# The bonus term of a time-mix layer: scale and offset applied where each direction's gate is taken up

## Chip, cores and metric

One core of one Trainium2 chip runs the whole program. The metric is device microseconds (us) of one launch: the median of three runs. The engines are called as the profile calls them: PE (TensorE matmul), PEld (its weight loads), DVE (VectorE), ACT (ScalarE), POOL (GpSimd), SP (SyncE, which here issues the DMAs).

## The reference, cut to what matters

The model is a trunk of two layers (a Mamba-2 mixer, then an RWKV-7 time mix), applied to 512 and 256 tokens of 1024 channels. Only the time mix is touched. For each of two directions z it computes a gate `a`, a key `k_dir` that depends on the gate, and, beside the recurrent scan, a bonus term, which sums over both directions:

```
a     = sigmoid(a0 + la @ a_up)                       # one gate for each direction z
k_dir = k * (1 + (a - 1) * k_a)
bonus = sum_over_z( sum_over_channels_of_a_head( r * k_dir * r_k ) ) * v
out   = ((y + bonus) * g) @ w_out
```

Both directions have the same r, k and r_k, so the sum over z needs the sum of the two gates only. With a = (1 + t) / 2, t being a tanh, the factor on r * k is rkk0 * (t_forward + t_backward) + rkk1, where rkk0 = k_a * r_k / 2 and rkk1 = (2 - k_a) * r_k are columns with one value for each channel.

## The kernel before

The 1024 channels of the time mix are eight blocks b of 128 channels (two heads of 64), with channels on the partitions and the 768 tokens along the free axis. For each block the program has five parts:

- `rwkv_in(b)`: the dense projections of k, r, v and g (fp32 as three fp32r products, lines 140 to 142 in `mm3`), shifted by a token (L737, L739) and stored to DRAM; q, k and r come back from there as `Wr`.
- `p1(b)`: six windows of 256 tokens, three for each direction. `p1_front` makes the decay (`ld`, `EP`) and the gate's tanh `ta` (L876); `p1_back` makes the matrices that the scan needs: `G` (POOL, L901 and L903), `KB` (ACT L897, DVE L898 and L904), `TD` and the rest of `G` from the product `ptd` (PE L912, DVE L914 and L917), `BK` (L922, L923). At its end stands the bonus term (L925 to L939).
- `rwkv_inverse(b)`: inverts the 24 triangular matrices of a block, mostly by a long row of small DVE operations (L963, L964), between DVE transposes (L956, L966, L967) and PE products (L977, L986).
- `chain_step(b, 0..7)`: the scan itself, a chain PE `pr` -> ACT `R` -> PE `pS` -> DVE and ACT `SV` -> PE `pz` -> DVE (L1017, L1031, L1056, L1057, L1065), with outputs `py` (L1039) copied to `Y` (L1076).
- `rwkv_final(b)`: the statistics of a block's output, `Y` added, centred, squared and scaled (POOL L1090, L1094, L1095, L1100; DVE L1093, L1097, L1098 and the reciprocal root `ng` in L103 to L108), then transposed by PE as `pf` (L1104), the bonus added (L1113), the gate g multiplied in (L1114).

The bonus in detail. The tile `ts` holds 768 tokens. Of the six windows three are the first to touch their 256 tokens (`first`), three the second. The first copies its `ta` to `ts` (ACT L927). The second adds its own `ta` (POOL L929), applies scale and offset rkk0 and rkk1 (DVE L930), multiplies by r and k (POOL L931, then L933 twice on 64 partitions), sums over each head with a product by `bones` (PE L935), multiplies by v (DVE L938) and stores to DRAM (L939). With eight blocks each of these lines runs 24 times, L933 and (as two passes) L935 48 times. The result is read back only in `rwkv_final(b)`, after the block's eight chain steps.

The order of the instructions on each engine isn't that of the code. After the program is written, a planner (`arrange`, `Program.schedule`) gives every instruction a cost by engine, operation and size, follows the dependencies, and lists the instructions of each engine by priority, in several passes with several settings; the best list by its own costs is fixed. Its lists are the order of issue on every engine, SP's DMAs included, so a changed cost or a vanished instruction at one place can move instructions anywhere in the program, the Mamba layer too. Dense products (the projections of later blocks, the output product) fill PE between the chain's small products.

Of the kernel before, what the change touches and what calls it, by code (L numbers as in the profile page):

```python
# [18 lines left out]
AF = mybir.ActivationFunctionType  # L19
ALU = mybir.AluOpType  # L20
# [28 lines left out]
def bc(ap, axis, n):  # L49
    a = ap.unsqueeze(axis)  # L50
    s = list(a.shape)
    s[axis] = n
    return a.to_broadcast(s)
# [6 lines left out]
class Trunk:  # L60
# [824 lines left out]
    def p1_back(self, b, w, z, o, a, ps4, first, W, En, ta, EP):  # L885
        nc = self.nc
        col = lambda t, i: t[:, i, b : b + 1]
        G, TD, PC = self.G, self.TD, self.PC[b]
        w4 = lambda ap: ap.rearrange("p (c t) -> p c t", t=C)
        m4 = bc(self.maskc[:, z].rearrange("p a t -> p (a t)"), 1, 4)  # L890
        flat = lambda ap: ap.rearrange("p c a t -> p c (a t)")
        tok = lambda ap: ap[..., ::-1] if z else ap
        pc = PC[:, 4 * w : 4 * w + 4]
        KB = self.wt([P, 4, 2, C], "KB")
        kv = KB.rearrange("p c j t -> p j c t")
        for j in range(2):
            nc.scalar.activation(kv[:, j], w4(ta), AF.Identity, scale=col(self.sx, 2 * j), bias=col(self.sx, 2 * j + 1))  # L897
        nc.vector.tensor_mul(kv, kv, tok(W[:, 0:2]).rearrange("p j (c t) -> p j c t", t=C))  # L898
        for h in range(2):
            hr = HR[h]  # L900
            nc.gpsimd.tensor_tensor(G[hr, ps4, h, 0, :], EP[hr, :, 0:C], w4(tok(W[hr, h])), op=ALU.mult)  # L901
            rho = G[hr, ps4, h, 1, :]
            nc.gpsimd.tensor_tensor(rho[..., ::-1] if z else rho, EP[hr, :, 1:], w4(tok(W[hr, 2])), op=ALU.mult)  # L903
        nc.vector.tensor_mul(kv, kv, bc(w4(En), 1, 2))  # L904
        nc.gpsimd.tensor_copy(pc, EP[:, :, C])


        ps = self.pt("s", [P, 2, 4, 2 * C], "ptd")
        for c in range(4):
            g = G[:, ps4.start + c * ps4.step]  # L910
            for h, j in ((0, 0), (1, 0), (0, 1), (1, 1)):
                nc.tensor.matmul(ps[HR[j], h ^ j, c], KB[HR[h], c, j], g[HR[h], h].rearrange("p a t -> p (a t)"),  # L912
                                 start=True, stop=True)
        nc.vector.tensor_tensor(flat(TD[:, ps4]), ps[:, 0], m4, op=ALU.mult)  # L914
        for h in range(2):
            hp = HR[1 - h]
            nc.vector.tensor_tensor(flat(G[hp, ps4, h]), ps[hp, 1], m4[hp], op=ALU.mult)  # L917
        for c in range(4):
            nc.scalar.activation(KB[:, c], KB[:, c], AF.Copy, scale=pc[:, c : c + 1])  # L919
        ps = self.pt("mi", [P, 4, 2 * C], "pbk")  # L920
        for c in range(4):
            nc.tensor.transpose(ps[:, c, :], KB[:, c].rearrange("p j t -> p (j t)"), self.ident)  # L922
        nc.scalar.copy(flat(self.BK[:, ps4]), ps)  # L923

        ts = self.ts[:, a : a + 256]  # L925
        if first:
            nc.scalar.copy(ts, tok(ta))  # L927
        else:
            nc.gpsimd.tensor_add(ts, ts, tok(ta))  # L929
            nc.vector.tensor_scalar(ts, ts, col(self.rkk, 0), col(self.rkk, 1), op0=ALU.mult, op1=ALU.add)  # L930
            nc.gpsimd.tensor_mul(ts, ts, W[:, 2])  # L931
            for h in range(2):
                nc.gpsimd.tensor_mul(ts[HR[h]], ts[HR[h]], W[HR[h], 1 - h])  # L933
            ps = self.pt("mi", [P, 256], "pbo")
            nc.tensor.matmul(ps, self.bones, ts, start=True, stop=True)  # L935
            v = self.rw.tile([P, 256], F32, tag="bo", bufs=1, name="v")
            nc.sync.dma_start(v, self.vin[b][:, a : a + 256])
            nc.vector.tensor_mul(ts, v, ps)  # L938
            nc.sync.dma_start(self.bod[b][:, a : a + 256], ts)  # L939
# [990 lines left out]
```

## Time and profile before

| what | value |
|---|---|
| median of three runs | 1632.25 us (1629.48 to 1632.38) |
| profiled execution, its own time | 1634.65 us |
| its span, first to last instruction | 1632.9 us |
| mean granted PE clock in it | 0.961 of full speed |
| PEld busy | 1293.0 us (79%) |
| DMA | 161.41 MB, mean 99 GB/s |
| time-mix layer | from about 785 us to the end |

An engine's busy time counts its instructions, not its waits, and a mean busy share mixes stages. A row of a group gives line, engine, operation, tiles out<-in, shapes and count, then its total us and the mean ns of one, then the idle time just before it with what ended that. In a timeline row stand the start, the duration, the engine and line, and in brackets the idle time before it and who ended that.

### The profile page before, as it was taken

The page shows a single profiled execution, that of the slowest core. Times are in us where ns is not written, and L with a number is a line of the kernel's source. Part 1 is how long each engine was busy: PE and PEld are TensorE (multiplying, and loading weights), DVE is VectorE, ACT ScalarE, POOL GpSimd, SP SyncE. Part 2 cuts the span into 40 slices and gives each one's busy share as a digit, 9 for nine tenths or more (in the row PEclk, how much of TensorE's full clock was granted, in tenths as well). Part 3 has the DMA queues.
Part 4 walks back from the last instruction along what each step waited for, and adds up shares of the span by engine and source line. Part 5 has one row for each costly group of instructions (what it writes and reads, how often), then busy time and mean ns, then how long its engine had stood idle before and what let it go on. Part 6 is the DMA issues. An engine that isn't in the chain of part 4 may idle for free. (4 is left out here: it accounts for less than half of the span.)

```text
span 1632.9 us, 39446 instructions
## 1 busy us (share of the span) xinstructions
PE 1526.4 (93%) x15210; PEld 1293.0 (79%) x15210; DVE 1361.9 (83%) x3031; ACT 850.8 (52%) x1980; POOL 723.5 (44%) x1007
## 2 busy tenths in 40 slices
PE   7999999999999899999979989999898999988996
PEld 6888888888988689998758767777777777776885
DVE  6779988888888885668688898989989898989768
ACT  4345444544545352424464757657574757656332
POOL 1168465574574661000070836446372836547210
PEclk9999999999999899999988898999899999979998
DMA  5110211212112044513334343443434344354332
GB/s 175 54 47 26 78 40 59 72 65 72 56 36 85 13 143 143 182 53 110 120 109 132 94 122 107 116 140 101 139 88 126 113 121 126 102 159 137 97 111 85
DMA packets 150316, 161.41 MB, mean 99 GB/s; under 512 B 39632, under 2 KB 106928, under 8 KB 150128
## 3 DMA queue, kind: packets, MB, share of 16 engines
q1 hardware_dynamic: 150128, 158.89, 32.5%
q8 instruction: 120, 1.97, 0.5%
q14 instruction: 68, 0.56, 0.1%
HBM read 121.43 MB, written 40.55 MB: 99 GB/s over the span
## 5 line engine op out<-in xcount | busy, mean ns | idle before, releaser
L140 PE MATMUL pj<-xh,whi 128*128 128x256 f32 (+1 forms) x1056 | 384.7, 365 | 18.9 <-ACT whi L122 10.2
L142 PE MATMUL pj<-xh,wlo 128*128 128x256 f32 (+1 forms) x1056 | 381.1, 361 | 4.3 <-DVE wlo L123 4.3
L141 PE MATMUL pj<-xl,whi 128*128 128x256 f32 (+1 forms) x1056 | 378.3, 358 | 1.4 <-DVE xl L136 1.4
L140 PEld LDWEIGHTS pj<-xh,whi 128*128 128x128 f32 x1056 | 207.0, 196 | 50.6 <-ACT whi L122 10.3
L142 PEld LDWEIGHTS pj<-xh,wlo 128*128 128x128 f32 x1056 | 207.3, 196 | 30.6 <-DVE wlo L123 6.2
L141 PEld LDWEIGHTS pj<-xl,whi 128*128 128x128 f32 x1056 | 207.7, 197 | 27.0 <-DVE xl L136 2.0
L122 ACT CAST whi<-wraw 128x512 fp32r<-128x512 f32 x213 | 131.4, 620 | 125.2 <-PE pj L141 61.7
L123 DVE TENSOR_TENSOR wlo<-wraw,whi 128x512 fp32r<-128x512 f32 x213 | 159.9, 755 | 33.3 <-ACT whi L122 31.1
L414 POOL TENSOR_SCALAR G<-past,ddt,dt 128x128 f32<-128x128 f32 x192 | 136.2, 720 | 84.6 <-DVE ddt L320 57.8
L140 PE MATMUL po<-whi,xh 128*128 128x256 f32 x528 | 151.8, 288 | 1.5 <-DVE acc L501 1.5
L142 PE MATMUL po<-whi,xl 128*128 128x256 f32 x528 | 152.0, 288 | 0.0
L141 PE MATMUL po<-wlo,xh 128*128 128x256 f32 x528 | 151.5, 287 | 0.0
L234 DVE SCALAR_TENSOR_TENSOR conv<-conv,convw 128x770 f32<-128x770 f32 x128 | 140.7, 1099 | 1.3
L140 PE MATMUL pz<-whi,xh 128*128 128x256 f32 x384 | 113.9, 297 | 1.1 <-DVE sz L258 1.1
L378 POOL TENSOR_TENSOR xw<-xB,dtws 128x256 f32<-128x256 f32 x64 | 53.5, 845 | 135.8 <-ACT xB L366 126.3
L901 POOL TENSOR_TENSOR G<-EP,Wr 64x256 f32<-64x256 f32 x96 | 88.5, 922 | 56.7 <-DMA Wr<-ind 36.3
L142 PE MATMUL pz<-whi,xl 128*128 128x256 f32 x384 | 111.5, 290 | 0.0
L141 PE MATMUL pz<-wlo,xh 128*128 128x256 f32 x384 | 111.1, 290 | 0.0
L140 PEld LDWEIGHTS po<-whi,xh 128*128 128x128 f32 x528 | 100.8, 191 | 2.9 <-DVE acc L501 1.9
L141 PEld LDWEIGHTS po<-wlo,xh 128*128 128x128 f32 x528 | 100.9, 191 | 1.5 <-issue 0.3
L142 PEld LDWEIGHTS po<-whi,xl 128*128 128x128 f32 x528 | 100.6, 191 | 1.5 <-DVE xl L136 0.2
L903 POOL TENSOR_TENSOR G<-EP,Wr 64x256 f32<-64x256 f32 x96 | 89.4, 931 | 1.7 <-ACT KB L919 0.8
(274 smaller groups left out, 3837.9 us busy)
## 6 DMA issues: line engine op xcount, KB each, us to landing
wraw<-in_r_w_in SPq DMA_DIRECT2D x72, 256.0 KB
Wr<-ind SPq DMA_DIRECT2D x48, 384.0 KB
wraw<-in_m_w_xbc SPq DMA_DIRECT2D x64, 256.0 KB
wraw<-in_m_w_z SPq DMA_DIRECT2D x32, 256.0 KB
wraw<-in_m_w_out SPq DMA_DIRECT2D x32, 256.0 KB
ydram<-yst SPq DMA_DIRECT2D x16, 384.0 KB
yraw<-ydram SPq DMA_DIRECT2D x24, 256.0 KB
ind<-k SPq DMA_DIRECT2D x32, 192.0 KB
```

The costliest lines, as they stand in the source:

```text
L122: nc.scalar.copy(hi, raw)
L123: nc.vector.tensor_sub(lo, raw, hi.bitcast(F32))
L140: mm(ps, ah, bh, start=first, stop=False)
L141: mm(ps, ah, bl, start=False, stop=False)
L142: mm(ps, al, bh, start=False, stop=last)
L234: nc.vector.scalar_tensor_tensor(acc, u[:, t : t + n], w[:, b, t : t + 1], acc, op0=ALU.mult, op1=ALU.add)
L378: nc.gpsimd.tensor_tensor(hv(xw), hv(xB[c][:, 0:256]), bc(self.dtws[:, c, z, hs], 2, 64), op=ALU.mult)
L414: nc.gpsimd.tensor_scalar(G[:, h, :], self.past, self.ddt[:, c, i : i + 1], self.dt[:, c, 0, i : i + 1], op0=ALU.mult, op1=ALU.add)
L901: nc.gpsimd.tensor_tensor(G[hr, ps4, h, 0, :], EP[hr, :, 0:C], w4(tok(W[hr, h])), op=ALU.mult)
L903: nc.gpsimd.tensor_tensor(rho[..., ::-1] if z else rho, EP[hr, :, 1:], w4(tok(W[hr, 2])), op=ALU.mult)
```

## The change

Scale and offset are applied where a gate is taken up. The first window's copy becomes an ACT activation with a scale and a bias for each partition (rkk0 and rkk1). The second window's two instructions become one DVE instruction, which multiplies `ta` by rkk0 and adds `ts`. POOL's addition is gone. All later lines stand one line higher (L931 becomes L930, L1104 becomes L1103).

```diff
         ts = self.ts[:, a : a + 256]
         if first:
-            nc.scalar.copy(ts, tok(ta))
+            nc.scalar.activation(ts, tok(ta), AF.Identity, scale=col(self.rkk, 0), bias=col(self.rkk, 1))
         else:
-            nc.gpsimd.tensor_add(ts, ts, tok(ta))
-            nc.vector.tensor_scalar(ts, ts, col(self.rkk, 0), col(self.rkk, 1), op0=ALU.mult, op1=ALU.add)
+            nc.vector.scalar_tensor_tensor(ts, tok(ta), col(self.rkk, 0), ts, op0=ALU.mult, op1=ALU.add)
             nc.gpsimd.tensor_mul(ts, ts, W[:, 2])
             for h in range(2):
                 nc.gpsimd.tensor_mul(ts[HR[h]], ts[HR[h]], W[HR[h], 1 - h])
```

`tok` reverses the tokens for the backward direction; `col(t, i)` is one column of 128 values.

The planner's lists change on all five engines. On POOL in block 0, where `p1(0)` makes its `G` with nothing else to run, there stood in the middle of the windows (rows in order of issue, tiles out<-in, then partitions by elements):

```order
L901 TENSOR_TENSOR G<-EP,Wr 64x4x64
L903 TENSOR_TENSOR G<-EP,Wr 64x4x64
L929 TENSOR_TENSOR ts<-ts,ta 128x256
L901 TENSOR_TENSOR G<-EP,Wr 64x4x64
L903 TENSOR_TENSOR G<-EP,Wr 64x4x64
L901 TENSOR_TENSOR G<-EP,Wr 64x4x64
L931 TENSOR_TENSOR ts<-ts,Wr 128x256
L903 TENSOR_TENSOR G<-EP,Wr 64x4x64
L933 TENSOR_TENSOR ts<-ts,Wr 64x256 x2
```

At the same place of POOL's list there now stands:

```order
L903 TENSOR_TENSOR G<-EP,Wr 64x4x64
L930 TENSOR_TENSOR ts<-ts,Wr 128x256
L905 COPY PC<-EP 128x4
L932 TENSOR_TENSOR ts<-ts,Wr 64x256
L901 TENSOR_TENSOR G<-EP,Wr 64x4x64
L903 TENSOR_TENSOR G<-EP,Wr 64x4x64
L901 TENSOR_TENSOR G<-EP,Wr 64x4x64
L903 TENSOR_TENSOR G<-EP,Wr 64x4x64
L932 TENSOR_TENSOR ts<-ts,Wr 64x256
```

The addition is gone from the run of `G`. The three products of the bonus (L930 and L932, before L931 and L933) are still in it; two of them now stand ahead of the four `G` of a window which they stood among or behind before.

The second place is DVE in the statistics of block 1, between the first and the second step of the reciprocal root (L108 writes `ngy` at the end of each step), while L963 and L964 invert the matrices of block 2, L123 splits weights and L739 shifts projections. The list before, up to the second L108:

```order
L123 TENSOR_TENSOR wlo<-wraw,whi 128x512
L963 TENSOR_TENSOR XN<-TL,tl 128x220
L106 TENSOR_TENSOR ngh<-ngy 128x12
L964 TENSOR_TENSOR tl<-tl,XN 128x11x20
L107 SCALAR_TENSOR_TENSOR ngh<-ngh,gv 128x12
L123 TENSOR_TENSOR wlo<-wraw,whi 128x512
L963 TENSOR_TENSOR XN<-TL,tl 128x210
L739 SCALAR_TENSOR_TENSOR rv<-pj_12315,hmu,rv 128x255
L964 TENSOR_TENSOR tl<-tl,XN 128x10x21
L739 SCALAR_TENSOR_TENSOR rv<-pj_12315,hmu,rv 128x255
L963 TENSOR_TENSOR XN<-TL,tl 128x198
L108 SCALAR_TENSOR_TENSOR ngy<-ngh,ngy 128x12
```

Between the same two steps the changed list has:

```order
L108 SCALAR_TENSOR_TENSOR ngy<-ngh,ngy 128x12
L962 TENSOR_TENSOR XN<-TL,tl 128x210
L106 TENSOR_TENSOR ngh<-ngy 128x12
L963 TENSOR_TENSOR tl<-tl,XN 128x10x21
L107 SCALAR_TENSOR_TENSOR ngh<-ngh,gv 128x12
L962 TENSOR_TENSOR XN<-TL,tl 128x198
L108 SCALAR_TENSOR_TENSOR ngy<-ngh,ngy 128x12
```

(L962 and L963 are now what L963 and L964 were.) Eleven rows stood between the two steps, now five: the two weight splits and the two shifts stand ahead of the first step, two rows of the inverse behind the second. None of these rows belongs to the bonus.

## The prediction

> **What bounds the kernel now.** I read the page's busy times first, then the stretches of the time-mix layer one by one, then who waits for whom, then single rows.
>
> ```profile
> PE 1526.4 (93%) x15210; PEld 1293.0 (79%) x15210; DVE 1361.9 (83%) x3031; ACT 850.8 (52%) x1980; POOL 723.5 (44%) x1007
> ```
>
> PE comes first over the whole span, POOL last. But the change lies after 785 us, so the stretches matter (columns: length, then busy us of each engine with its instructions, granted PE clock, DMA share, GB/s):
>
> ```profile
> core 0: us, PE busy (x) PEld busy (x) DVE busy (x) ACT busy (x) POOL busy (x), PEclk, DMA share, GB/s
> 814.00:850.00 36.00, 25.69 (x284) 19.81 (x283) 31.86 (x45) 24.32 (x64) 31.01 (x45) 0.81 0.35 103
> 1000.00:1500.00 500.00, 464.46 (x6252) 369.34 (x6252) 449.48 (x1009) 326.85 (x817) 274.45 (x405) 0.94 0.41 119
> 1155.00:1170.00 15.00, 10.89 (x44) 8.37 (x43) 14.56 (x48) 2.64 (x6) 2.20 (x2) 0.77 0.46 141
> 785.00:1633.00 848.00, 767.26 (x9638) 623.35 (x9636) 729.77 (x1752) 498.69 (x1240) 386.04 (x573) 0.93 0.40 117
> ```
>
> Three regimes. From 814 to 850 us, the first block's windows, POOL and DVE are nearly full and PE waits. In the blocks that follow PE and DVE share the bound (93% and 90% of 1000 to 1500 us) and POOL has 45% to spare. In the last 15 us of a block's statistics (1155 to 1170) DVE is full, PE has 4 us of holes and its clock is at 0.77. The waits say which hole is largest (who waited for whom, us, times, longest):
>
> ```profile
> PE pf L1104 <- POOL Y L1100: 18.1, 7, 4.3
> PE tl L977 <- DVE TC L967: 4.2, 3, 2.5
> PE ptd L912 <- POOL G L903: 1.1, 3, 0.4
> POOL Y L1100 <- DVE ngy L108: 43.1, 4, 12.5
> POOL ts L931 <- DVE ts L930: 13.3, 9, 3.6
> ```
>
> PE's largest wait in this layer is for the normalised output before its transposition, 18.1 us in seven blocks, and that waits for the reciprocal root on DVE. The bonus appears only as a wait of POOL, which isn't the bound. For the matrices `G` PE waits 1.1 us in all. So the bonus itself is off the path nearly everywhere; what it does is take time on engines, and occupy a place in lists.
>
> **POOL: 24 additions go.** The groups of the old and the neighbouring lines:
>
> ```profile
> L929 POOL TENSOR_TENSOR ts<-ts,ta 128x256 f32<-128x256 f32 x24 | 20.1, 837 | 3.1 <-ACT ta L876 2.0
> L930 DVE TENSOR_SCALAR ts<-ts,rkk 128x256 f32<-128x256 f32 x24 | 12.1, 503 | 0.6 <-POOL ts L929 0.5
> L927 ACT COPY ts<-ta 128x256 f32<-128x256 f32 x24 | 9.6, 403 | 1.6 <-DMA bod<-ts 1.5
> L897 ACT ACTIVATE KB<-ta,sx 128x256 f32<-128x256 f32 x96 | 53.6, 597 | 7.0 <-PE pbk L922 6.7
> L938 DVE TENSOR_TENSOR ts<-v,pbo 128x256 f32<-128x256 f32 x24 | 9.9, 412 | 2.0 <-PE pbo L935 1.3 <-PE pS L1017 0.3
> L739 DVE SCALAR_TENSOR_TENSOR rv<-pj,hmu,rv 128x255 f32<-128x255 f32 x32 | 15.2, 475 | 0.1
> ```
>
> POOL loses 24 x 0.837 = 20.1 us. Where POOL is 55% busy that is free; in the first block it isn't. There POOL runs back to back:
>
> ```profile
> 824.82 0.69 POOL L903 TENSOR_TENSOR G<-EP,Wr 64x256 f32<-64x256 f32 x1
> 825.58 0.72 POOL L929 TENSOR_TENSOR ts<-ts,ta 128x256 f32<-128x256 f32 x1
> 826.27 1.12 POOL L901 TENSOR_TENSOR G<-EP,Wr 64x256 f32<-64x256 f32 x1
> ```
>
> ```profile
> L929 POOL TENSOR_TENSOR ts<-ts,ta x24: 722/732/1892, 825.6 to 1492.0; 128x256 f32<-128x256 f32 x24
> ```
>
> One addition of 0.72 us stands among the `G`; the other two of the block follow the last `G`. PE, TD, the inverse and the first chain step wait for these `G`. The new list moves two of the bonus's products ahead of one window's `G`, but the last `G` of the block has the same products ahead of it as before, less the addition. Term one: **-0.7 us**. A loss is excluded, since nothing was put into this run; at most it is the longest addition's 1.9 us (least, median, largest ns stand in the last row), if DVE, the other full engine, gives way too.
>
> **DVE: one row for one row.** The old instruction costs 24 x 0.503. The trace has no such operation on two SBUF tiles; the nearest are L938 at 0.412 (two inputs, no pointer) and L739 at 0.475 (a pointer, one input from PSUM). I take L739, being the same operation, and the spread that the old one had above its own median:
>
> ```profile
> L930 DVE TENSOR_SCALAR ts<-ts,rkk x24: 364/406/867, 827.5 to 1501.3; 128x256 f32<-128x256 f32 x24
> L904 DVE TENSOR_TENSOR KB<-KB,ld x48: 654/1052/1254, 814.8 to 1489.5; 128x512 f32<-128x512 f32 x48
> L901 POOL TENSOR_TENSOR G<-EP,Wr x96: 671/946/2503, 814.2 to 1490.2; 64x256 f32<-64x256 f32 x96
> ```
>
> 0.475 + (0.503 - 0.406) = 0.57, so 24 x 0.07 = +1.7 us. Against it stands what the vanished additions took from others: L904 takes between 0.65 and 1.25 us, and POOL's L901 between 0.67 and 2.5, because the two engines hinder each other on SBUF. L904 (mean 0.941, below) loses 48 x (0.941 - 0.654) = 13.8 us over 386 us of POOL; with the two rows
>
> ```profile
> L904 DVE TENSOR_TENSOR KB<-KB,ld 128x512 f32<-128x512 f32 x48 | 45.2, 941 | 0.7
> L898 DVE TENSOR_TENSOR KB<-KB,Wr 128x512 f32<-128x512 f32 x48 | 42.9, 894 | 10.0 <-DMA Wr<-ind 7.7 <-ACT KB L897 1.7
> ```
>
> and the same least time, L898 adds 48 x 0.24 = 11.5 us: 25.3 / 386 = 0.066 us for each us of POOL, 1.3 us for 20.1. Term two: 1.7 - 1.3, of which only a part is on the path: **0**, ends -3.5 (the 0.412 row and the whole relief) and +1.7. The new row waits for ACT's `ta` and for the first window's `ts`, both older than POOL's sum, for which DVE waited 0.5 us in all; so nothing behind it on DVE (most often `TD` or a scan of the next window) gets a wait. No DMA is added or taken away.
>
> The Trainium skill, "SBUF — State Buffer", section "SBUF: two separate sides", says that a VectorE instruction with two SBUF inputs and a GpSimd instruction that reads SBUF exclude each other for a whole instruction. By this rule the new row, with `ta` and `ts` from SBUF, is such a holder 24 times; the trace shows the hindrance, though L930 at up to 0.87 us was hindered with one input already. Its result is a rival below.
>
> **ACT.** The copy becomes an activation with two pointers, as L897 is: 24 x (0.597 - 0.403) = +4.7 us on an engine that is 65% busy from 1000 to 1500 us. Its cover is that slack. In the new list six of the 24 have one of the chain's or the output's copies within the next two rows, so the loss is at most 6 x 0.19 = 1.2 us. Term three: **0**, end +1.2; a gain is excluded, the row only grows.
>
> **What the planner moved.** The lists differ on every engine; three differences can be priced. First, PE turns between the tiled products (L912, L1017, L1039) and full ones 522 times in the old list, 508 times in the new. The price is in four rows:
>
> ```profile
> 1580.41 0.28 PE L142 MATMUL po<-whi,xl 128*128 128x256 f32 x1
> 1580.53 0.28 PE L140 MATMUL po<-whi,xh 128*128 128x256 f32 x1
> 1580.74 0.33 PE L1039 MATMUL py<-SV,TD 64*64 64x64 f32 x4
> 1581.00 0.39 PE L141 MATMUL po<-wlo,xh 128*128 128x256 f32 x1
> 1581.22 0.28 PE L142 MATMUL po<-whi,xl 128*128 128x256 f32 x1
> ```
>
> Dense rows start every 0.12 us; into the tiled row it takes 0.21, out of it the next 0.22: about 0.1 for a turn. Term four: 14 x 0.1 = **-1.4 us**, ends 0 (they fall into holes) and -2.8.
>
> Second, the statistics. From the sums (L1093) to the root's last row the old DVE list has 41 rows in block 0 and 295 in seven blocks, the new one 259.
>
> ```profile
> 963.81 0.95 DVE L1093 TENSOR_REDUCE gm<-Y 128x12 f32<-128x768 f32 x1 [0.39 <-POOL Y L1090]
> 977.35 0.16 DVE L108 SCALAR_TENSOR_TENSOR ngy<-ngh,ngy 128x12 f32<-128x12 f32 x1
> ```
>
> 13.5 us for 41 rows, 0.33 each: 36 rows fewer bring the output 11.9 us earlier in all, against 18.1 us of waiting, less what covers it: the dense rows between the last `py` and the first `pf` come to 79.7 us before and 78.8 now, by the spacings 0.12 above and 0.23 for 512 columns:
>
> ```profile
> 1058.05 0.39 PE L140 MATMUL pj<-xh,whi 128*128 128x512 f32 x1
> 1058.27 0.39 PE L141 MATMUL pj<-xl,whi 128*128 128x512 f32 x1
> ```
>
> That would be -11.0. But DVE is full there, and the rows taken out stand behind the root, where PE waits for the inverse next (L977, 4.2 us already). So most of the wait should move from `pf` to the inverse and not vanish: I take some eighth part, **-1.5 us**, with the ends -11 and +4.3 (the slower rival).
>
> Third, the end. Behind the last chain step the new lists have 28 PE rows and, on DVE, three weight splits (0.75 by the row below) and two accumulations (0.42) less; they now run before it.
>
> ```profile
> L123 DVE TENSOR_TENSOR wlo<-wraw,whi 128x512 fp32r<-128x512 f32 x213 | 159.9, 755 | 33.3 <-ACT whi L122 31.1
> L501 DVE SCALAR_TENSOR_TENSOR acc<-acc,po 128x256 f32<-128x256 f32 x72 | 30.0, 417 | 28.4 <-PE po L142 26.8 <-DMA acc<-x2d 1.3
> ```
>
> The full DVE of the last 30 us saves 3.1, the chain before it meets 28 x 0.12 = 3.4 of dense work: **0**, ends -3.1 and +3.4.
>
> **Sum**: -0.7 - 1.4 - 1.5 = -3.6 us. The profiled execution took 1634.65 us, span 1632.9, so the same execution would take 1631.05; it lies 2.4 above the median 1632.25, which becomes 1628.65, **1628.7 us**. A measurement of this kernel tells about 0.2%, 3.3 us, from no change.
>
> **Rivals.**
>
> *The moved waits come back, no change.* For it: DVE is 97% busy in the statistics, and the turns may fall into the holes of PE. Against: POOL's place in block 0 is real. Only term one is left: 1631.6.
>
> *Faster by far: POOL and DVE exclude each other, and the hole at `pf` closes.* By the lock of whole instructions, each of the 24 additions that meets a holder costs DVE up to 0.73, half on average: 24 x 0.37 = 8.8 us of DVE, of which the 10% of the layer's time that PE idles says little is on the path. With a third of the 11 us of statistics it would be 1628.7 - 0.9 - 2.2 = 1625.6; with all 11 and no return, 1618. For it: L904's median of 1.05 against a least of 0.65. The rule named above would make it so, if the new rows weren't holders too.
>
> *Slower: the statistics are no earlier, and blocks 1 and 3 have less to cover them.* Dense rows ahead of `pf` come to 10.9, 11.7, 11.4, 12.3, 11.2, 10.9, 11.3 us by block before, and 10.7, 10.2, 13.2, 10.2, 10.7, 12.1, 11.6 now. If POOL's and ACT's steps, and not DVE's rows, set when the output is ready, the four blocks that lose cover pay 4.3 us, and those that gain get nothing where the inverse is next to be late: 1632.25 + 4.3 = 1636.6. It decides once the statistics gain less than some 0.6 us a block. A hole also costs clock:
>
> ```profile
> 1066.25 0.27 PE L801 MATMUL prs<-ident,nky 128*12 128x128 f32 x1 [1.77 <-DVE rv L739]
> 1067.90 0.63 PE L140 MATMUL pj<-xh,whi 128*128 128x512 f32 x1
> 1068.33 0.63 PE L141 MATMUL pj<-xl,whi 128*128 128x512 f32 x1
> ```
>
> After 1.77 us without work, dense rows start every 0.43 us instead of 0.23: ten such rows cost 2 us more. That the change doesn't do what it says is excluded: the new list has no addition.
>
> **Numbers.** Forecast 0.36; faster by far 0.09; no change 0.30; slower 0.25. Faster by over 0.2% (below 1629.0) is the first two, 0.45; within, 0.30; slower 0.25. The range reaches from the whole statistics nearly kept (1620) to the slower rival with one block's lost clock (1638.6, so 1639); the Mamba layer's reordering, which I can't price, lies within it.
>
> **What would show it.** The group `ts<-ta,rkk,ts` on DVE at 0.48 to 0.6 us, the ACT row at about 0.6; POOL about 703 us; `PE pf <- POOL Y` under 18 us with `PE tl <- DVE TC` above 4.2; the first chain step about 0.7 us earlier after `p1(0)`. I am wrong if the difference lies before 785 us, or if `pf` waits more than 20 us, or if the new DVE row takes over 0.8.

## The result, and the profile after

Twenty runs of each kernel on the same chips: 1631.68 us before (median; 1627.16 to 1639.26), 1625.99 us after (1618.83 to 1630.79). The ratio, over all runs, is 0.9964, with a 95% interval of 0.995 to 0.9979: 0.36% faster, by the medians 5.7 us where 3.6 was forecast. The profiled execution took 1625.2 us, its span is 1623.4 us.

The page's busy times after the change, for the span and then three stretches of the time-mix layer (the columns are those of before: length, busy us of PE, PEld, DVE, ACT, POOL with instructions, granted clock, DMA share, GB/s):

```profile
PE 1519.9 (94%) x15210; PEld 1289.9 (79%) x15210; DVE 1355.5 (83%) x3031; ACT 853.7 (53%) x1980; POOL 698.3 (43%) x983
```

```profile
814.00:850.00 36.00, 29.44 (x312) 23.01 (x310) 33.52 (x48) 26.84 (x68) 29.93 (x40) 0.95 0.46 131
1000.00:1500.00 500.00, 464.83 (x6216) 371.09 (x6209) 449.46 (x1027) 326.31 (x814) 255.84 (x391) 0.94 0.42 120
785.00:1623.00 838.00, 760.83 (x9638) 620.35 (x9638) 724.98 (x1752) 502.89 (x1241) 364.31 (x549) 0.94 0.41 118
```

POOL is 25.2 us less busy, 20.1 of it the additions. From 1000 to 1500 us PE and DVE are as full as they were, to half a microsecond: relieving POOL changed nothing in how full the two bounds are. Over the span PE is 6.5 us less busy with the same 15210 rows, to which the end of the account comes back. The new rows, and the neighbours that share SBUF with POOL (line and group, then total us, mean ns, idle time before):

```profile
L927 ACT ACTIVATE ts<-ta,rkk 128x256 f32<-128x256 f32 x24 | 14.5, 602 | 1.6 <-DMA bod<-ts 1.6
L929 DVE SCALAR_TENSOR_TENSOR ts<-ta,rkk,ts 128x256 f32<-128x256 f32 x24 | 13.2, 554 | 4.8 <-ACT ta L876 4.8
L904 DVE TENSOR_TENSOR KB<-KB,ld 128x512 f32<-128x512 f32 x48 | 45.2, 942 | 0.5
L898 DVE TENSOR_TENSOR KB<-KB,Wr 128x512 f32<-128x512 f32 x48 | 43.2, 901 | 6.7 <-DMA Wr<-ind 5.4 <-ACT KB L897 0.7
```

The two costs are near the forecast (0.60 and 0.57). Not foreseen are the 4.8 us that DVE waits for ACT's `ta` ahead of its new row. L904 and L898 are no shorter than before. The waits that the forecast spoke of (us, times, longest):

```profile
PE pf L1103 <- POOL Y L1099: 17.0, 7, 3.6
PE tl L976 <- DVE TC L966: 7.5, 6, 3.6
POOL ts L930 <- DVE ts L929: 18.5, 8, 3.9
```

The wait at the transposition lost 1.1 us, the one for the inverse gained 3.3. So where did the 9.5 us between the two spans come from? Some 3.8 of them are the choice of executions: the profiled one before was 3.0 us slower than its kernel's median, the one after 0.8 faster than its own. For the rest, ACT's row `R`, at the start of every chain step, serves as a mark of time in the layer. Before, at the first step of blocks 0, 3 and 7 and at the last step of all:

```profile
871.58 0.39 ACT L1031 ACTIVATE R<-pr 128x256 f32<-128x256 f32 x1
1148.25 0.38 ACT L1031 ACTIVATE R<-pr 128x256 f32<-128x256 f32 x1
1519.18 0.39 ACT L1031 ACTIVATE R<-pr 128x256 f32<-128x256 f32 x1 [0.46 <-PE pr L1017]
1583.76 0.28 ACT L1031 ACTIVATE R<-pr 128x128 f32<-128x128 f32 x1 [0.29 <-PE pr L1017]
```

and after:

```profile
867.61 0.39 ACT L1030 ACTIVATE R<-pr 128x256 f32<-128x256 f32 x1
1139.64 0.36 ACT L1030 ACTIVATE R<-pr 128x256 f32<-128x256 f32 x1
1507.13 0.38 ACT L1030 ACTIVATE R<-pr 128x256 f32<-128x256 f32 x1
1578.37 0.28 ACT L1030 ACTIVATE R<-pr 128x128 f32<-128x128 f32 x1 [0.19 <-PE pr L1016]
```

The lead is 4.0 us at the first chain step, 8.6 at block 3, 12.1 at block 7, then only 5.4 at the last step, and 9.5 at the end. In between, at block 1's first step, the changed kernel is 3.1 us behind (964.53 against 961.38). A lead that comes and goes like this doesn't follow the bonus, which every block has. That asks whether the instructions or the planner's lists made the difference.

### The profile page after: what moved, and what is told of

It is laid out like the page before. It is cut to its first block, busy times and chain, and to the rows that moved or that the text cites. A ratio compares the mean times of both kernels' runs of the same rounds, so it can differ in the third digit from the quotient of the medians.

```text
span 1623.4 us, 39367 instructions
## 1 busy us (share of the span) xinstructions
PE 1519.9 (94%) x15210; PEld 1289.9 (79%) x15210; DVE 1355.5 (83%) x3031; ACT 853.7 (53%) x1980; POOL 698.3 (43%) x983
## 4 chain that ended last, share of the span: by engine, by line
PE 71%; DVE 16%; ACT 4%; POOL 3%; issue 2%; DMA 2%; SPq 0%; DVEq 0%; ACTq 0%; POOLq 0%
PE pj L140 10%; PE pj L141 9%; PE pj L142 9%; PE py L1038 3%; PE ptd L912 3%; PE po L140 3%; PE po L141 3%; PE po L142 3%; PE pz L140 3%; PE pz L141 2%; PE pz L142 2%; PE pr L1016 2%; PE pS L1016 2%; DVE tl L963 2%; PE pst L380 2%
## 5 line engine op out<-in xcount | busy, mean ns | idle before, releaser
L140 PE MATMUL pj<-xh,whi 128*128 128x512 f32 (+1 forms) x1056 | 382.9, 363 | 19.5 <-ACT whi L122 10.4
L141 PE MATMUL pj<-xl,whi 128*128 128x512 f32 (+1 forms) x1056 | 374.0, 354 | 0.9 <-DVE xl L136 0.9
L142 PE MATMUL pj<-xh,wlo 128*128 128x512 f32 (+1 forms) x1056 | 373.5, 354 | 0.3
L123 DVE TENSOR_TENSOR wlo<-wraw,whi 128x512 fp32r<-128x512 f32 x213 | 155.6, 734 | 36.4 <-ACT whi L122 35.2
L414 POOL TENSOR_SCALAR G<-past,ddt,dt 128x128 f32<-128x128 f32 x192 | 129.8, 686 | 88.8 <-DVE ddt L320 56.8
L901 POOL TENSOR_TENSOR G<-EP,Wr 64x256 f32<-64x256 f32 x96 | 83.8, 872 | 52.2 <-DMA Wr<-ind 40.2
L903 POOL TENSOR_TENSOR G<-EP,Wr 64x256 f32<-64x256 f32 x96 | 87.3, 910 | 2.5 <-PE py L1038 0.9
```

Source lines behind the costliest of these rows:

```text
L123: nc.vector.tensor_sub(lo, raw, hi.bitcast(F32))
L140: mm(ps, ah, bh, start=first, stop=False)
L141: mm(ps, ah, bl, start=False, stop=False)
L142: mm(ps, al, bh, start=False, stop=last)
L414: nc.gpsimd.tensor_scalar(G[:, h, :], self.past, self.ddt[:, c, i : i + 1], self.dt[:, c, 0, i : i + 1], op0=ALU.mult, op1=ALU.add)
```

## The experiments

Theory A: the vanished POOL work and the lighter sharing of SBUF make the gain. Theory B, its rival: the planner's new lists make it, and the instructions are worth nothing by themselves. Every kernel of this section issues finished lists that are stored in it; the edits shown say how these lists were made. Every ratio below is against the kernel before on the same chip, over all runs, and can differ a little from the ratio of two medians.

**One: new instructions, old lists.** The changed code, with this in place of the planner's result (the name stands for the stored lists):

```diff
-    for line in prog.schedule().values():
+    for line in LISTS_OF_THE_KERNEL_BEFORE_LESS_24_ADDITIONS:
```

> The changed instructions, issued on every engine in the order of the kernel before (its lists, less the 24 additions; the new DVE row stands where the old one stood). Theory A, the gain comes from the vanished POOL work and the lighter sharing of SBUF between POOL and DVE: most of the 5.7 us appears here, ratio 0.997 or less, and the first chain step of block 0 comes 2 to 4 us earlier. Theory B, the gain comes from the planner's new lists: ratio 0.999 to 1.001, POOL still 20 us less busy, and the largest wait of PE, for the normalised output, stays near 18 us.

Measured: 1.0006 (0.9988 to 1.0023; medians 1633.65 us against 1631.72). Its busy times, the two DVE rows that share SBUF with POOL, and its waits:

```profile
PE 1523.7 (93%) x15210; PEld 1290.0 (79%) x15210; DVE 1360.4 (83%) x3031; ACT 854.3 (52%) x1980; POOL 705.6 (43%) x983
```

```profile
L904 DVE TENSOR_TENSOR KB<-KB,ld 128x512 f32<-128x512 f32 x48 | 43.9, 915 | 0.7
L898 DVE TENSOR_TENSOR KB<-KB,Wr 128x512 f32<-128x512 f32 x48 | 40.7, 847 | 9.3 <-DMA Wr<-ind 7.3 <-ACT KB L897 1.6
```

```profile
PE pf L1103 <- POOL Y L1099: 18.3, 7, 4.2
PE tl L976 <- DVE TC L966: 4.2, 3, 2.5
```

Theory A falls: POOL is 17.9 us less busy, the two DVE rows are 3.5 us shorter (84.6 against 88.1), and the time stays. The two waits are those of the kernel before. The lead at the first chain step, which theory A had expected too, was there all the same:

```profile
868.56 0.38 ACT L1030 ACTIVATE R<-pr 128x256 f32<-128x256 f32 x1
```

That is 3.0 us ahead of the kernel before, in a kernel whose median is no better. How much one place moves from execution to execution can be read from three kernels that issue the same list up to this step, the changed one and experiments eight and nine below: they reach it at 867.61, 870.87 and 869.91 us. A lead of three or four microseconds there, in single executions, can't be told from that.

**Two and five: old instructions, new lists.** The code of before, the changed kernel's lists, and the 24 additions put in: in experiment two just ahead of each window's product, in five as early as the gate allows.

> The instructions of the kernel before, issued in the order of the changed kernel; each of the 24 POOL additions stands just ahead of its window's first product, or up to eight POOL rows earlier where that order would otherwise lock up. Theory A (vanished POOL work): near the kernel before, ratio 0.999 to 1.002. Theory B (new lists): near the changed kernel, ratio 0.995 to 0.998.

> The instructions of the kernel before in the order of the changed kernel again, but each POOL addition as early in POOL's list as its gate allows, where in the second experiment it stood just ahead of the window's first product. Theory B (the lists decide, the instructions do not): near the changed kernel, ratio 0.995 to 0.999. Theory C (the new lists can only be followed by the new instructions, since in some windows the new DVE row stands directly behind the gate, with no room for an addition on POOL in between): DVE still waits for POOL's sum, 5 to 15 us of it against 44 in the second experiment, and the ratio lies between 1.000 and 1.008.

Measured: two 1.0187 (1.016 to 1.0214), far above both bands; five 1.0086 (1.0068 to 1.0104), its middle just above theory C's band. DVE's waits for POOL's sum, in two and in five:

```profile
DVE ts L930 <- POOL ts L929: 44.0, 18, 5.8
```

```profile
DVE ts L930 <- POOL ts L929: 10.3, 6, 2.9
```

Neither half of the comparison is clean: in some windows the lists leave no room for an addition, and an instruction that waits in DVE's order holds up the chain's copies and `TD` behind it. In five the additions also stand among the `G`, and 10.3 us of wait don't explain all of its 14 us of loss. So the old instructions lose by these lists with the additions in either of these two places. That fits theory C, by which the lists suit the new instructions only, but no other place was tried.

**Three, four, six, seven, eleven, twelve: the same instructions, planned again.** To the planner's assumed cost of every instruction of one engine 1 ns is added, which says nothing about the chip; DVE in three and four, POOL in six and seven, ACT in eleven and twelve; the instructions of before in three, six and eleven, the changed ones in the others.

```diff
+        for i in range(n):
+            if self.eng[i] == "DVE" and self.cost[i]:
+                self.cost[i] += 1.0
```

> The instructions of the kernel before, planned again with 1 ns added to the cost that the planner assumes for every DVE instruction, which says nothing about the chip. Theory B (lists decide): the time moves by some 2 to 8 us either way, as far as the change moved it. Theory A: ratio within 0.2% of 1.

> The changed instructions, planned again with 1 ns added to the planner's cost of every DVE instruction. Theory A (the gain belongs to the instructions): ratio 0.996 again, within 0.15%. Theory B (it belongs to one list): anywhere from 0.993 to 1.002, 2 us or more from the changed kernel.

> The instructions of the kernel before, planned again with 1 ns added to the planner's cost of every POOL instruction. Theory B: a draw from the lists that the planner may give, ratio anywhere from 0.994 to 1.010. Theory D (the list of the kernel before is a lucky draw): above 1.002 like the first such replan.

> The changed instructions, planned again with 1 ns added to the planner's cost of every POOL instruction. Theory B: a draw, 0.994 to 1.010. If the changed instructions let the planner find better lists in general, this one should beat the replans of the kernel before (1.004) and lie below 1.000.

> The instructions of the kernel before, planned again with 1 ns added to the planner's cost of every ACT instruction. If the lists are draws, 0.996 to 1.008; the mean of the four lists with the old instructions then comes out within 0.2% of that of the four with the new ones.

> The changed instructions, planned again with 1 ns added to the planner's cost of every ACT instruction. If the lists are draws, 0.996 to 1.008, and the mean of four lists equals that of the old instructions. If the change is worth 0.3% in itself, the mean of the four is 0.3% below that of the old ones, which asks for 0.99 here.

| lists | old instructions | new instructions |
|---|---|---|
| as planned | 1 | 0.9964 (0.995 to 0.9979) |
| DVE + 1 ns | 1.0043 (1.0027 to 1.006) | 1.0073 (1.0049 to 1.0098) |
| POOL + 1 ns | 1.0018 (1.0002 to 1.0035) | 1.0016 (0.9998 to 1.0033) |
| ACT + 1 ns | 1.0024 (1.0011 to 1.0037) | 1.0005 (0.9989 to 1.0021) |
| mean | 1.0021 | 1.0015 |

A nanosecond in the planner moves the chip's time by up to 1.1% between two lists of the same instructions (0.9964 and 1.0073). The means of four lie 0.07% apart. With so wide a spread four draws can't exclude that the change is worth 0.3% either way on average, but the changed kernel's own result is the best of its four lists, and none of the six new plans is better than the kernel before. The signs that the forecast priced don't foretell the time either: experiment three's list has 480 turns of PE between tiled and full products against 522 before, and is slower; experiment six waits little at the transposition,

```profile
PE pf L1104 <- POOL Y L1100: 8.4, 5, 2.1
```

8.4 us against 18.1, and is slower too.

**Eight, nine, ten: spliced lists.** The changed instructions throughout; the issue order is one kernel's up to a chain step and the other's from there on.

> The changed instructions in the changed kernel's order up to the first chain step of block 7, and from there on in the order of the kernel before. In the profiles block 7 with the end took 113.7 us before and 116.3 after, so if the difference belongs to this part of the lists, the kernel gains 2 to 3 us on the changed one: ratio 0.994 to 0.995. If block 7 only takes what the earlier part of the list has left it, nothing is gained: 0.996 to 0.998.

> The changed instructions; the changed kernel's order up to the first chain step of block 3, the order of the kernel before from there on. In the profiles the changed kernel is 8.6 us ahead at that step and 9.5 at the end, so if the gain lies in the order of blocks 0 to 2, all of it appears here: ratio 0.994 to 0.9975. If it is spread over the whole layer, or a list is only good as a whole: 0.998 to 1.001.

> The counterpart: the changed instructions in the order of the kernel before up to the first chain step of block 3, in the changed kernel's order from there on. If the gain lies in blocks 0 to 2: ratio 0.999 to 1.002, no gain. If it lies later: 0.994 to 0.998.

Measured: eight 0.9955 (0.9938 to 0.9971), nine 0.9985 (0.9971 to 0.9999), ten 0.9998 (0.9984 to 1.0013). Eight is the fastest kernel measured, 1623.65 us, but its interval and that of the changed kernel overlap almost wholly. Its profile shows the end of the list. The changed kernel and experiment eight, each from block 7's first `R` to the last `R`, and from there to the end:

```profile
1507.13:1578.37 71.24, 64.62 (x899) 57.17 (x897) 45.27 (x138) 26.04 (x66) 14.98 (x23) 0.93 0.38 107
1578.37:1623.40 45.03, 29.29 (x246) 27.79 (x240) 40.52 (x174) 13.37 (x35) 0.00 (x0) 0.87 0.22 80
```

```profile
1506.27:1572.46 66.19, 60.64 (x872) 52.81 (x870) 43.93 (x131) 23.37 (x63) 14.16 (x23) 0.97 0.38 108
1572.46:1621.30 48.84, 33.35 (x270) 31.07 (x266) 43.99 (x179) 15.03 (x38) 0.00 (x0) 0.90 0.24 83
```

At block 7 the two, with one list so far, are within 1 us of each other (1507.13 and 1506.27). Then the old order is 5.0 us quicker through the chain and 3.8 slower behind it: the changed kernel has 27 more PE rows ahead of the chain's end, which go with a longer first part and a shorter second, and 1.2 us are left, in one execution of each. Nine and ten were to find the gain's place and did not: the new order up to block 3, the Mamba layer's included, is worth about 0.15% alone, that from block 3 on nothing that can be told (0.02%), both together 0.36%. Whether the list is only good as a whole or the intervals hide the rest stays open.

## Why the prediction was right, and which steps of it were not

The time lay within the range, and the sign and the size of the forecast held. But no term of the sum was borne out as it was priced, so that the size came out was luck. The measured 1626.0 us even lies nearer to the 1625.6 of the rival "faster by far" than to 1628.7, again without its mechanism.

*POOL's additions, -0.7 us.* Not seen. The first and the last `G` of block 0, before and after:

```profile
814.25 1.05 POOL L901 TENSOR_TENSOR G<-EP,Wr 64x256 f32<-64x256 f32 x1 [13.55 <-PE pj L142]
...
840.92 0.68 POOL L903 TENSOR_TENSOR G<-EP,Wr 64x256 f32<-64x256 f32 x1
```

```profile
814.82 0.96 POOL L901 TENSOR_TENSOR G<-EP,Wr 64x256 f32<-64x256 f32 x1 [13.53 <-DMA Wr<-ind]
...
841.64 1.14 POOL L903 TENSOR_TENSOR G<-EP,Wr 64x256 f32<-64x256 f32 x1
```

27.4 us before and 28.0 after, and the first start, which is no earlier, shows that the lead didn't come from ahead of the layer. The time of the addition was taken up by rows that POOL was held up in, one of which is described at the end. There was also little to be had: the 1.1 us that the prediction gives as PE's wait for `G` in all is that from 850 us on. With block 0's windows it is, before and after,

```profile
PE ptd L912 <- POOL G L903: 2.8, 5, 1.1
PE ptd L912 <- POOL G L903: 2.6, 6, 0.9
```

With the old lists the bound is experiment one's: at best 0.12%, 2 us, for everything that the instructions do.

*DVE and ACT, 0.* The durations were right, 0.554 and 0.602 us against 0.57 and 0.597, and so was that they cost no time. That nothing gets a wait was wrong: DVE's 4.8 us for `ta` come with the new lists; with the old ones the new row waits 0.1. The relief on SBUF was 1.3 us in the forecast and 3.5 in experiment one, which gained nothing by it; in the changed kernel, in its other order, L904 and L898 together take 88.4 us against 88.1. The lock of "faster by far" was to be worth 0.9 us, which the bound of 2 us can't exclude; its larger part, that the hole at `pf` closes, did not come, for 17.0 of 18.1 us are left.

*PE's turns, -1.4 us.* This step failed: a count of turns was priced as if the rest stayed. The other lists differ from the old one by far more than their turns: 42 fewer turns, in experiment three, came with 0.43% more time, 36 fewer, in twelve, with 0.05% more, and two more, in nine, with 0.15% less.

*The statistics, -1.5 us of a possible 11.* Their first half held: from the sums to the root's last row the seven blocks took 97.4 us before and 85.4 after, 12.0 us less where 11.9 was forecast. What covers it was wrong: the forecast left it almost as it was. The stretches from the sums (L1093; L1092 after the change) to the first `pf`, seven blocks added up, before and after:

```profile
sum 109.06, PE 82.08 PEld 67.85 DVE 107.10 ACT 28.77 POOL 24.22; mean PE 11.73 PEld 9.69 DVE 15.30 ACT 4.11 POOL 3.46
sum 97.10, PE 74.86 PEld 62.59 DVE 95.18 ACT 27.78 POOL 23.56; mean PE 10.69 PEld 8.94 DVE 13.60 ACT 3.97 POOL 3.37
```

The stretches are 12.0 us shorter, but PE is also 7.2 us less busy in them (in part by its clock, 0.90 in two of the seven before and at least 0.96 after), where the forecast had counted on 0.9 us less of dense rows. So PE's idle time there fell by 4.7 us only. The wait for the normalised output fell by 1.1 and that for the inverse rose by 3.3; the two together were 22.3 us before and 24.5 after. That the earlier statistics pushed the inverse back on a full DVE would fit, but wasn't tested. Nor do these stretches make the time: they are shorter still, 96.0 and 93.5 us, in experiments six and twelve, which are no faster than the kernel before. The slower rival, blocks 1 and 3 with less cover, did not come either: the wait at the transposition fell.

*The end, 0.* Block 7's chain became 6.7 us longer (64.6 to 71.2), what follows 4.1 shorter (49.1 to 45.0): +2.6 in one execution of each, within the ends given, on the side of a loss.

So the rival "no change" describes what the instructions do in the old order, and the gain belongs to the new order, which the forecast priced through three visible differences, none of which foretells the time. What makes the better list better was not settled. PE's waits don't tell it: in the time-mix layer they are 61.9 us in all (the sum of PE's rows in the view of waits) against 67.4 before, and 79.0 and 78.7 in experiments three and four, but 61.7 in experiment twelve, which is no faster than the kernel before. Its page:

```profile
PE 1531.9 (94%) x15210; PEld 1300.9 (80%) x15210; DVE 1352.4 (83%) x3031; ACT 852.7 (52%) x1980; POOL 697.3 (43%) x983
```

The same rows keep PE busy 12.0 us longer than in the changed kernel, and the span is 12.6 longer; the mean granted clock was 0.956 in that execution, 0.966 in the changed kernel's. Between the kernel before (0.961) and the changed one, too, 6.5 of the 9.5 us are PE's busy time. Over all runs the mean clock is 0.962 for the kernel before (35 runs, taken beside experiments nine to twelve), 0.967 for the changed one, 0.970 for experiments eight and nine, and between 0.954 and 0.963 for all others: the three kernels that gained are the three with the highest clock. Among the 20 runs of the changed kernel alone, 0.001 more clock went with 0.8 us less time, among the 35 of the kernel before with 0.5. By these slopes, an estimate, the difference in clock (0.0046) goes with some 2.5 to 4 of the 5.7 us. Whether the order raises the clock, or both follow from something else in it, was not tested; it is the outcome of a list and no way to foretell it.

## What to carry to other kernels

Where a planner orders everything, test a small edit with the old order fixed before believing its time: here, in the old order, the instructions were worth nothing that could be told (0.12% faster to 0.23% slower), and the 0.36% belonged to a list that a nanosecond in the planner's costs throws away. Don't price a new order by counting one thing in it, and don't read a lead of 3 us at one place of two single executions as a cause. Read the granted clock of all runs beside the waits: here it set the three faster kernels apart, and the waits didn't. If an order is good, keep the order itself: it can be stored, and it survived a splice.

## What the runs showed of the hardware

A small row of POOL can be held up through several DVE rows. The copy of 128x4 values at L905 has a median of 0.19 us and took 1.95 us once in block 0 of the changed kernel; POOL's row and DVE's of the same time:

```profile
827.40 1.95 POOL L905 COPY PC<-EP 128x4 f32<-128x4 f32 x1
```

```profile
827.50 0.67 DVE L878 TENSOR_TENSOR_SCAN ld<-scanm,ld 128x256 f32<-128x256 bf16 x1
828.10 0.66 DVE L898 TENSOR_TENSOR KB<-KB,Wr 128x512 f32<-128x512 f32 x1
828.68 0.68 DVE L878 TENSOR_TENSOR_SCAN ld<-scanm,ld 128x256 f32<-128x256 bf16 x1
829.28 0.66 DVE L914 TENSOR_TENSOR TD<-ptd,maskc 128x512 f32<-128x512 f32 x1
```

It ended at 829.35, as the first row with an input from PSUM began; the three rows before it read two SBUF tiles each and ran close to their shortest (0.67 and 0.66 us are the least of L878 and L898). The Trainium skill, "SBUF — State Buffer", section "SBUF: two separate sides", lets whichever instruction starts first keep the shared ports for its whole length; this row agrees that DVE rows with two SBUF inputs hold POOL off, and shows three in a row doing so, though by the record POOL's row had begun 0.1 us before the first. Whether that start is the moment at which a row gets the ports, no run here shows.
